# First mixer's shift and scale: fp32 products of two columns, or fp32r products of four columns of high and low parts

## The chip, the cores and the metric

One Trainium2 chip, one of its cores. The metric is the device time of one execution in microseconds (us); smaller is better. Several executions are timed, and one more is profiled.

## The reference

Two blocks of layers over 512 tokens of width 1024, with a context of 256 tokens beside them in the first. What matters here stands at the very start: a vector c (for the tokens) and a vector c_ctx (for the context) give the shift and the scale of the first mixer's input.

```
ada        = silu(c)     @ ada_w[0] + ada_b[0]     (1024 -> 12 x 512)
ada_ctx    = silu(c_ctx) @ ada_w[0] + ada_b[0]
modulate(t, shift, scale) = t * (1 + scale) + shift
h, hc      = modulate(x, ...), modulate(ctx, ...)
p, pc      = h @ w_in, hc @ w_in                   (then scans, convolutions, feed-forward, a second block)
```

Shift and scale of the first mixer are the column blocks q = 0..3 of `ada_w[0]` (q 0 and 1 shift, q 2 and 3 scale; an even q serves the first half of the 1024 features, an odd one the second half). All is float32. The dense layers of the kernel reach that with fp32r: each operand is cut into a high part (a cast) and a low part (the rest), and three products of parts are summed.

## The kernel before

**Order of the program.** `Kern.consts` (L343) sets constants and calls `ada_begin` (L598), which loads c and c_ctx, and takes silu into `sv`, 128 x 8 x 2: for each of 8 blocks k of 128 features one column for c and one for c_ctx. Then `mixer` (L1236) calls `modulated_inputs` (L679). A scheduler sets the order on each engine; `order` rows below show it. Each engine works through its own list in order, SP's list is the queue of most loads.

**The head.** `modulated_inputs` runs: `ada_head(2)`, `ada_head(0)`; loads of the first half of x and ctx (`load(0)`, L699); the weight loads of the first two dense layers, `dt` (`wdt`, 48 columns) and the first block of `wxbc` (128 columns, here called xbc8); `modulate(0)` (L702 to L711); `ada_head(1)` and `ada_head(3)` in turns; `load(1)`; the first four blocks of those two dense layers; `modulate(1)`.

**`ada_head(q)`** (L607) takes the weights of one q as four pairs of blocks, 128 x 1024 float32, 512 KB each. A pair lands in a buffer that is a `wraw`, a `wh` or a `wl` of the weight pool by turns (three of each, nine in all). For each of the 8 blocks one fp32 product, `sv[:, k]` (two columns) times 128 x 512 weights, sums into `pr` (2 x 512, L617). The sum goes to SBUF (`adarow`, L624), four small transposes turn it into columns (`pt`, L626), and two vector instructions add the bias into `hm` (L629).

**`modulate(half)`** for four blocks each: ScalarE makes t * scale + shift in place (L707), VectorE the same for the context (L709), ScalarE casts both to their high parts `ch` and `xh` (L710), VectorE and GpSimd (for the context) subtract for the low parts `xl` and `cl` (L711).

**The dense layers** (`dense2`, L737) load weights by `wload` (L381): land in `wraw`, ScalarE casts to `wh` (L394), VectorE and GpSimd subtract for `wl` (L396, L397). `mm3` (L403) makes the three products (L405 to L407). `wh` and `wl` have three buffers each, and a layer keeps its pair until the product of its last block, k = 7.

```
raw = self.wp.tile([P, 1024], F32, name="wraw", tag="wraw", bufs=3)
wh = self.wp.tile([P, 1024], F32R, name="wh", tag="wh", bufs=3)
wl = self.wp.tile([P, 1024], F32R, name="wl", tag="wl", bufs=3)
```

**After the head** `ssd_dt` (L770) takes the sum of `dt` through some 20 small steps on VectorE and ScalarE; TensorE's first instruction that needs it is the transpose `ptd` (L815). Meanwhile TensorE goes on with the other `wxbc` layers.

Of the kernel before, what the change touches and what calls it, by code (L numbers as in the profile page):

```python
# [10 lines left out]
F32 = mybir.dt.float32  # L11
F32R = mybir.dt.float32r
# [5 lines left out]
P = 128  # L18
T = 512
TC = 256  # L20
D = 1024
KD = 8
# [293 lines left out]
class Kern:  # L316
# [26 lines left out]
    def consts(self):  # L343
        nc, cst = self.nc, self.cst
# [5 lines left out]
        nc.gpsimd.affine_select(self.ident, self.ident, pattern=[[1, P]], base=0, channel_multiplier=-1,  # L350
                                compare_op=OP.is_equal, fill=0.0)
        self.ones = cst.tile([P, 1], F32, name="ones")
        nc.vector.memset(self.ones, 1.0)
# [244 lines left out]
    def ada_begin(self):  # L598
        nc = self.nc
        cv = self.cst.tile([P, KD, 2], F32, name="cv")  # L600
        nc.scalar.dma_start(cv, self.i["cvec"])
        self.sv = self.cst.tile([P, KD, 2], F32, name="sv")
        nc.scalar.activation(self.sv, cv, AF.Silu)
        self.m = [self.cst.tile([P, 48], F32, name=f"m{l}") for l in range(2)]
        self.mc = self.cst.tile([P, 16], F32, name="mc")

    def ada_head(self, q):  # L607

        nc = self.nc
        pr = self.x("pr")  # L610
        for k in range(0, KD, 2):
            self.nraw += 1
            raw = self.wp.tile([P, 1024], F32, name="wraw", tag=("wraw", "wh", "wl")[self.nraw % 3], bufs=3)
            nc.sync.dma_start(raw, self.i["ada0"][q, :, k:k + 2].rearrange("p k c -> p (k c)"))
            for j in range(2):
                r = raw[:, j * 512:(j + 1) * 512]
                nc.tensor.matmul(pr[:2], self.sv[:, k + j], r, start=k + j == 0, stop=k + j == KD - 1)  # L617
            yield
# [4 lines left out]
        row = self.t("adarow")  # L623
        nc.vector.tensor_copy(row[:2], pr[:2])  # L624
        for j in range(4):
            nc.tensor.transpose(pt[:, j], row[:2, j * P:(j + 1) * P], self.ident[:2, :2])  # L626
        hm = self.hm[q] = self.ctxp.tile([P, 2, 4], F32, name=f"hm{q}")
# [608 lines left out]
    def mixer(self):  # L1236
        nc = self.nc
# [11 lines left out]
        pb = self.pool("ssdb", 1, es=ess, **right)  # L1249
        chain = lambda *g: (c for x in g for c in x)  # L1250
        dt, s0 = self.dense2(self.i["wdt"], 0, 48), self.ssd_inputs(0, pa)
        self.modulated_inputs([dt, s0])
# [1285 lines left out]
```

## Time and profile before

| | |
|---|---|
| time, median of 3 runs | 2649.17 us (2646.44 to 2653.3) |
| the profiled execution | 2647.25 us, span of its trace 2645.5 us |
| TensorE (PE) busy | 2562.8 us, 97% of the span |
| VectorE (DVE), ScalarE (ACT), GpSimd (POOL) | 68%, 43%, 30% |
| DMA | 264.30 MB, mean 100 GB/s |

Rows of the trace name an engine, a source line (L617), the tiles written and read (out<-in), and a shape; times are in us from the span's start. "[0.76 <-DVE dtv L798]" is idle time of the engine before the row, and what ended it. A 128x512 fp32 product stands as two records in the trace.

### The profile page before, as it was taken

To read this page: it belongs to the slowest core of one execution; us is meant where nothing else is said; L and a number is where in the kernel's file an instruction comes from. 1 tells how busy PE (TensorE), PEld (TensorE's weight loads), DVE (VectorE), ACT (ScalarE), POOL (GpSimd) and SP (SyncE) were. 2 spreads that over 40 slices of the span, in tenths; PEclk is the share of its full clock that TensorE was granted. 3 is DMA by queue.
4 is the path that set the end of the run, shared out by engine and by line. 5 is a ranking of instruction groups with operands and counts; after the bars stand their busy time and mean duration, and the time that the engine had idled before them with its cause. 6 is when DMAs were issued, how large, how long until landed. Compare 5 with 4: busy or idle time off the path is not lost. (4 is left out here: it accounts for less than half of the span.)

```text
span 2645.5 us, 37506 instructions
## 1 busy us (share of the span) xinstructions
PE 2562.8 (97%) x14044; PEld 2163.8 (82%) x14044; DVE 1787.2 (68%) x3239; ACT 1128.8 (43%) x1958; POOL 786.1 (30%) x818
## 2 busy tenths in 40 slices
PE   8999999999999999999989999999999999999998
PEld 3877778989779888788888888888887889988887
DVE  3787866775777988868977888557544777644422
ACT  3545433333425333226875433226545445433322
POOL 2133312231343211325635221342234112322231
PEclk9999999999999999999989999999999999999999
DMA  7223225441353333752202333333223102333332
GB/s 257 70 68 116 72 79 165 132 132 48 110 185 105 96 96 95 252 178 75 78 1 64 112 96 96 96 95 100 67 72 91 33 9 80 113 98 99 97 94 76
DMA packets 94181, 264.30 MB, mean 100 GB/s; under 512 B 11008, under 2 KB 15424, under 8 KB 94000
## 3 DMA queue, kind: packets, MB, share of 16 engines
q1 hardware_dynamic: 87136, 249.00, 30.7%
q10 hardware_dynamic: 4752, 6.63, 0.7%
q0 software_dynamic: 2112, 6.29, 0.7%
q8 instruction: 110, 1.80, 0.3%
q14 instruction: 71, 0.58, 0.1%
HBM read 253.39 MB, written 7.44 MB: 99 GB/s over the span
## 5 line engine op out<-in xcount | busy, mean ns | idle before, releaser
L405 PE MATMUL acc<-xh,wl 128*128 128x512 f32 (+2 forms) x2056 | 778.0, 379 | 9.5 <-ACT xh L1624 3.1
L406 PE MATMUL acc<-xh,wh 128*128 128x512 f32 (+2 forms) x2056 | 767.8, 374 | 0.0
L407 PE MATMUL acc<-xl,wh 128*128 128x512 f32 (+2 forms) x2056 | 765.3, 375 | 1.1 <-POOL xl L379 0.8
L397 POOL TENSOR_TENSOR wl<-wraw,wh 128x256 fp32r<-128x256 f32 (+2 forms) x318 | 345.1, 1086 | 1158.4 <-ACT wh L394 1055.2
L394 ACT CAST wh<-wraw 128x1024 fp32r<-128x1024 f32 (+2 forms) x318 | 326.4, 1028 | 531.3 <-PE acc L407 318.2
L396 DVE TENSOR_TENSOR wl<-wraw,wh 128x768 fp32r<-128x768 f32 (+2 forms) x318 | 349.2, 1099 | 180.8 <-ACT wh L394 149.5
L405 PEld LDWEIGHTS acc<-xh,wl 128*128 128x128 f32 (+1 forms) x2056 | 392.1, 191 | 74.0 <-issue 4.7
L407 PEld LDWEIGHTS acc<-xl,wh 128*128 128x128 f32 (+1 forms) x2056 | 389.9, 191 | 72.0 <-issue 2.5
L406 PEld LDWEIGHTS acc<-xh,wh 128*128 128x128 f32 (+1 forms) x2056 | 392.1, 191 | 57.2 <-issue 1.9
L2456 DVE SCALAR_TENSOR_TENSOR cacc<-acc,pk,cacc 128x441 f32<-128x441 f32 (+2 forms) x352 | 243.8, 693 | 27.9 <-ACT cacc L2447 18.6
L405 PE MATMUL acc<-gh,wl 128*128 128x512 f32 (+1 forms) x594 | 221.9, 374 | 0.0
L407 PE MATMUL acc<-gl,wh 128*128 128x512 f32 (+1 forms) x594 | 221.1, 372 | 0.0
L406 PE MATMUL acc<-gh,wh 128*128 128x512 f32 (+1 forms) x594 | 220.7, 372 | 0.0
L642 DVE SCALAR_TENSOR_TENSOR adaacc<-adaraw,sv,adaacc 128x512 f32<-128x512 f32 x140 | 116.5, 835 | 31.7 <-DMA adaraw<-in_ada 29.7
L406 PEld LDWEIGHTS acc<-gh,wh 128*128 128x128 f32 x594 | 113.0, 190 | 21.4
L407 PEld LDWEIGHTS acc<-gl,wh 128*128 128x128 f32 x594 | 112.8, 190 | 21.3
L405 PEld LDWEIGHTS acc<-gh,wl 128*128 128x128 f32 x594 | 112.9, 190 | 21.0
L1543 DVE SCALAR_TENSOR_TENSOR pc<-up,pk,pc 128x512 f32<-128x512 f32 x119 | 89.7, 754 | 3.3
L2400 DVE SCALAR_TENSOR_TENSOR cacc<-acc,pk,cacc 128x511 f32<-128x511 f32 (+1 forms) x44 | 33.0, 750 | 70.0 <-ACT cacc L2398 69.2
L1138 ACT COPY kcur<-kk 128x512 f32<-128x512 f32 x56 | 37.3, 666 | 92.7 <-DVE kk L1162 92.6
L1148 PE MATMUL pa<-qq,kcur 128*128 128x128 f32 x448 | 64.6, 288 | 6.5 <-DVE qq L1160 6.3
L1164 POOL TENSOR_TENSOR tot<-tot 128x256 f32<-128x256 f32 (+5 forms) x48 | 26.9, 561 | 145.0 <-DVE qq L1160 134.6
(673 smaller groups left out, 4633.3 us busy)
## 6 DMA issues: line engine op xcount, KB each, us to landing
wraw<-in_wup SPq DMA_DIRECT2D x132, 512.0 KB, 3.6
adaraw<-in_ada SPq DMA_DIRECT2D x160, 256.0 KB, 3.4
wraw<-in_wdn SPq DMA_DIRECT2D x48, 512.0 KB, 3.6
wraw<-in_wc SPq DMA_DIRECT2D x24, 512.0 KB, 3.6
wraw<-in_wdn SPq DMA_DIRECT2D x24, 384.0 KB, 3.1
wraw<-in_ada SPq DMA_DIRECT2D x16, 512.0 KB, 5.7
wraw<-in_wf SPq DMA_DIRECT2D x16, 512.0 KB, 3.8
wraw<-in_wo SPq DMA_DIRECT2D x16, 512.0 KB, 3.7
```

The costliest lines, as they stand in the source:

```text
L394: nc.scalar.copy(wh[:, :n], raw[:, :n])
L396: nc.vector.tensor_sub(wl[:, :c], raw[:, :c], wh[:, :c])
L397: nc.gpsimd.tensor_sub(wl[:, c:n], raw[:, c:n], wh[:, c:n])
L405: mm(acc, wl, xh, start=first, stop=False)
L406: mm(acc, wh, xh, start=False, stop=False)
L407: mm(acc, wh, xl, start=False, stop=last)
L642: nc.vector.scalar_tensor_tensor(a, r, self.sv[:, k, 0:1], a, op0=OP.mult, op1=OP.add)
L1138: nc.scalar.copy(t.rearrange("p (a b c) -> p a b c", b=2, c=m), self.alt(kk, 0)(m))
L1148: mm(pa[:, s], kcur[:, s], self.alt(qq, 1)(m, c * P, P), start=True, stop=True)
L1543: nc.vector.scalar_tensor_tensor(pc, at(j0 + j), w(j0 + j, n), pc, op0=OP.mult, op1=OP.add)
L2400: nc.vector.scalar_tensor_tensor(a[:, d:], pg[:, :T - d], self.col("gcw", (2 - d) * KF + j), a[:, d:], op0=OP.mult, op1=OP.add)
L2456: nc.vector.scalar_tensor_tensor(o, g3[:, r0 + dy:r1 + dy, c0 + dx:c1 + dx], w, o, op0=OP.mult, op1=OP.add)
```

## The change

`sv4` holds for each block four columns: the high parts of the two, then their low parts. The weights of a pair are cut as those of a dense layer are: ScalarE casts each half (128 x 512) to `wh`, VectorE or GpSimd subtracts to `wl`; GpSimd takes the first half of the pairs k = 0 and k = 4, VectorE all else. Two fp32r products per block, of `wh` and of `wl` with all four columns, sum into `pr` (4 x 512). The four transposes become four products with `sel4`, 4 x 2, that also add the rows of high and low parts. Pairs now land in `wraw` alone, or (every second one) as two loads of 256 KB in two of the four `er` tiles, which the scan uses later.

```diff
+        self.sel4 = cst.tile([4, 2], F32, name="sel4")
+        nc.vector.tensor_add(self.sel4, self.ident[0:4, 0:2], self.ident[0:4, 2:4])
...
+        self.sv4 = self.cst.tile([P, KD, 4], F32R, name="sv4")
+        nc.scalar.copy(self.sv4[:, :, 0:2], self.sv)
+        nc.vector.tensor_sub(self.sv4[:, :, 2:4], self.sv, self.sv4[:, :, 0:2])
...
-            raw = self.wp.tile([P, 1024], F32, name="wraw", tag=("wraw", "wh", "wl")[self.nraw % 3], bufs=3)
-            nc.sync.dma_start(raw, self.i["ada0"][q, :, k:k + 2].rearrange("p k c -> p (k c)"))
+            if self.nraw % 2:
+                t = self.wp.tile([P, 1024], F32, name="wraw", tag="wraw", bufs=3)
+                nc.sync.dma_start(t, self.i["ada0"][q, :, k:k + 2].rearrange("p k c -> p (k c)"))
+                raw = t[:, :512], t[:, 512:]
+            else:
+                raw = [self.erp.tile([P, T], F32, name="er", bufs=4) for _ in range(2)]
+                for j in range(2):
+                    nc.sync.dma_start(raw[j], self.i["ada0"][q, :, k + j])
+            wh = self.wp.tile([P, 1024], F32R, name="wh", tag="wh", bufs=3)
+            wl = self.wp.tile([P, 1024], F32R, name="wl", tag="wl", bufs=3)
             for j in range(2):
-                r = raw[:, j * 512:(j + 1) * 512]
-                nc.tensor.matmul(pr[:2], self.sv[:, k + j], r, start=k + j == 0, stop=k + j == KD - 1)
+                s = slice(j * 512, (j + 1) * 512)
+                nc.scalar.copy(wh[:, s], raw[j])
+                (nc.vector if j or k % 4 else nc.gpsimd).tensor_sub(wl[:, s], raw[j], wh[:, s])
+                nc.tensor.matmul(pr[:4], self.sv4[:, k + j], wh[:, s], start=k + j == 0, stop=False)
+                nc.tensor.matmul(pr[:4], self.sv4[:, k + j], wl[:, s], start=False, stop=k + j == KD - 1)
...
-        nc.vector.tensor_copy(row[:2], pr[:2])
+        nc.vector.tensor_copy(row[:4], pr[:4])
         for j in range(4):
-            nc.tensor.transpose(pt[:, j], row[:2, j * P:(j + 1) * P], self.ident[:2, :2])
+            nc.tensor.matmul(pt[:, j], row[:4, j * P:(j + 1) * P], self.sel4, start=True, stop=True)
```

The list of ScalarE around the end of `modulate(0)`. Before (L710 casts of the last block, then at once what comes ahead of `modulate(1)`, L707 on `yc`; L800 belongs to `ssd_dt`):

```order
17 L707 ACTIVATE xin<-xin,hm_206,hm_179 128x512
18 L710 CAST ch<-xin 128x256
19 L710 CAST xh<-xin 128x512
20 L800 ACT_TABLE_LOAD
21 L800 ACTIVATE ea<-pk 48x1
22 L707 ACTIVATE yc<-yc,hm_325,hm_315 128x512
```

Of the change, with the semaphores that a row waits for in brackets (PE, DVE and Pool are other engines' progress, DMAHW a load; L724 and L727 are the lines of `modulate`, L631 the casts of `ada_head`):

```order
36 L727 CAST xh<-xin 128x512 [waits Activation_49]
37 L631 CAST wh<-wraw 128x512 [waits DMAHW3_49,PE_49]
38 L631 CAST wh<-wraw 128x512
39 L631 CAST wh<-er 128x512 [waits DVE_49,DMAHW4_49,PE_49,Pool_49]
40 L631 CAST wh<-er 128x512 [waits DMAHW5_49]
41 L631 CAST wh<-wraw 128x512 [waits DVE_49,DMAHW6_49,PE_49,Pool_49]
42 L631 CAST wh<-wraw 128x512
43 L631 CAST wh<-er 128x512 [waits DMAHW7_49,DVE_49,PE_49]
```

Sixteen casts of `ada_head(1)` and `ada_head(3)` now stand between the two halves of `modulate`, and the first cast of each pair waits for TensorE, VectorE or GpSimd as well as for its load.

TensorE in the same stretch, before (L617 the fp32 products, L405 to L407 those of `dt`):

```order
12 L617 MATMUL pr<-wraw,sv 2x512 x6
13 L405 MATMUL acc<-xh,wl 48x512
14 L406 MATMUL acc<-xh,wh 48x512
15 L617 MATMUL pr<-wraw,sv 2x512 x6
16 L407 MATMUL acc<-xl,wh 48x512
17 L405 MATMUL acc<-ch,wl 48x256
18 L406 MATMUL acc<-ch,wh 48x256
19 L617 MATMUL pr<-wraw,sv 2x512 x2
```

Of the change (L633 and L634 the new products, L407 to L409 those of the dense layers, 128 rows for xbc8):

```order
61 L633 MATMUL pr<-wh,sv_78 4x512
62 L408 MATMUL acc<-ch,wh 48x256
63 L409 MATMUL acc<-cl,wh 48x256
64 L634 MATMUL pr<-wl,sv_78 4x512
65 L633 MATMUL pr<-wh,sv_78 4x512
66 L407 MATMUL acc<-xh,wl 128x512
67 L408 MATMUL acc<-xh,wh 128x512
68 L634 MATMUL pr<-wl,sv_78 4x512
69 L409 MATMUL acc<-xl,wh 128x512
70 L633 MATMUL pr<-wh,sv_78 4x512
71 L407 MATMUL acc<-ch,wl 128x256
72 L408 MATMUL acc<-ch,wh 128x256
```

The products of `ada_head` now stand among the first halves of both dense layers, where before only half of `dt` stood among them.

TensorE behind the last transposes, before (the end of `dt`'s first half, then xbc8's first half, of which row 35 is the first product):

```order
30 L626 MATMUL pt<-ident,adarow 128x2 x4
31 L407 MATMUL acc<-xl,wh 48x512
32 L405 MATMUL acc<-ch,wl 48x256
33 L406 MATMUL acc<-ch,wh 48x256
34 L407 MATMUL acc<-cl,wh 48x256
35 L405 MATMUL acc<-xh,wl 128x512
```

Of the change:

```order
115 L643 MATMUL pt<-sel_87,adarow 128x2 x8
116 L407 MATMUL acc<-ch,wl 48x256
117 L408 MATMUL acc<-ch,wh 48x256
118 L407 MATMUL acc<-ch,wl 128x256
119 L409 MATMUL acc<-cl,wh 48x256
120 L408 MATMUL acc<-ch,wh 128x256
121 L407 MATMUL acc<-xh,wl 48x512
122 L408 MATMUL acc<-xh,wh 48x512
```

Behind the transposes nothing is left that needs only the first half of the inputs; `dt` and xbc8 then go side by side.

## Rows read from the trace of the kernel before

**Rows 1.** The page: span, and busy time of the engines.

```profile
span 2645.5 us, 37506 instructions
PE 2562.8 (97%) x14044; PEld 2163.8 (82%) x14044; DVE 1787.2 (68%) x3239; ACT 1128.8 (43%) x1958; POOL 786.1 (30%) x818
```

**Rows 2.** Stretches of the head: busy us of engines, granted clock, DMA share, GB/s.

```profile
core 0: us, PE busy (x) PEld busy (x) DVE busy (x) ACT busy (x) POOL busy (x), PEclk, DMA share, GB/s
0.00:20.00 20.00, 13.89 (x31) 2.74 (x32) 1.65 (x12) 1.50 (x2) 0.70 (x6) 1.00 0.92 341
20.00:46.00 26.00, 22.96 (x74) 5.97 (x72) 9.05 (x20) 9.40 (x17) 5.07 (x6) 1.00 0.90 323
46.00:60.00 14.00, 14.00 (x81) 11.37 (x80) 9.79 (x15) 10.81 (x17) 6.10 (x6) 1.00 0.27 84
60.00:74.00 14.00, 13.24 (x90) 11.03 (x88) 9.96 (x19) 6.64 (x9) 2.19 (x2) 1.00 0.19 58
74.00:82.00 8.00, 8.00 (x33) 7.21 (x34) 6.91 (x19) 3.61 (x9) 0.05 (x1) 0.57 0.43 132
```

**Rows 3.** Timeline of TensorE, the products of ada_head(2) and ada_head(0).

```profile
5.24 9.15 PE L617 MATMUL pr<-wraw,sv 128*2 128x512 f32 x16 [5.24 <-ACT sv L603]
15.56 7.03 PE L617 MATMUL pr<-wraw,sv 128*2 128x512 f32 x16
```

**Rows 4.** Timeline, from the last sum of ada_head(0) through modulate(0).

```profile
22.63 0.68 DVE L624 COPY adarow<-pr 2x512 f32<-2x512 f32 x1 [0.47 <-PE pr L617]
23.36 0.40 PE L626 MATMUL pt<-ident,adarow 2*128 2x2 f32 x4 [0.77 <-DVE adarow L624]
24.36 0.22 DVE L629 SCALAR_TENSOR_TENSOR hm<-pt,pk 128x4 f32<-128x4 f32 x2
24.55 0.81 ACT L707 ACTIVATE xin<-xin,hm,hm 128x512 f32<-128x512 f32 x1 [1.10 <-DVE hm L629]
25.27 0.39 ACT L710 CAST ch<-xin 128x256 fp32r<-128x256 f32 x1
25.56 0.61 ACT L710 CAST xh<-xin 128x512 fp32r<-128x512 f32 x1
26.08 0.81 ACT L707 ACTIVATE xin<-xin,hm,hm 128x512 f32<-128x512 f32 x1
```

**Rows 5.** Timeline, casts of the weights of dt and xbc8.

```profile
21.15 0.51 ACT L394 CAST wh<-wraw 128x384 fp32r<-128x384 f32 x1 [15.96 <-DMA wraw<-in_wdt]
22.40 1.04 ACT L394 CAST wh<-wraw 128x1024 fp32r<-128x1024 f32 x1 [0.74 <-DMA wraw<-in_wxbc]
```

**Rows 6.** Lines L391, L392, L379: 128x512 cast and subtractions, ns min/median/max.

```profile
L391 ACT CAST wh<-wraw x36: 508/617/626, 790.7 to 2620.3; 128x512 fp32r<-128x512 f32 x30, 128x384 fp32r<-128x384 f32 x6
L392 DVE TENSOR_TENSOR wl<-wraw,wh x36: 548/684/1778, 792.6 to 2620.9; 128x512 fp32r<-128x512 f32 x30, 128x384 fp32r<-128x384 f32 x6
L379 POOL TENSOR_TENSOR gl<-u,gh x27: 1307/1313/2023, 855.1 to 2503.8; 128x512 fp32r<-128x512 f32 x27
```

**Rows 7.** Timeline, subtractions of POOL and DVE that overlap.

```profile
27.26 0.74 POOL L711 TENSOR_TENSOR cl<-xin,ch 128x256 fp32r<-128x256 f32 x1 [0.81 <-ACT ch L710]
27.74 0.81 DVE L711 TENSOR_TENSOR xl<-xin,xh 128x512 fp32r<-128x512 f32 x1 [0.53 <-ACT xh L710]
...
53.08 0.96 DVE L396 TENSOR_TENSOR wl<-wraw,wh 128x768 fp32r<-128x768 f32 x1
53.12 1.51 POOL L397 TENSOR_TENSOR wl<-wraw,wh 128x256 fp32r<-128x256 f32 x1 [0.74 <-ACT wh L394]
```

**Rows 8.** Timeline, the end of ada_head(1) and (3), and modulate(1)'s start.

```profile
43.10 1.28 DVE L624 COPY adarow<-pr 2x512 f32<-2x512 f32 x2 [11.50 <-PE pr L617]
45.66 0.23 DVE L629 SCALAR_TENSOR_TENSOR hm<-pt,pk 128x4 f32<-128x4 f32 x2 [0.93 <-PE pt L626]
45.86 0.82 ACT L707 ACTIVATE yc<-yc,hm,hm 128x512 f32<-128x512 f32 x1 [1.94 <-DVE hm L629]
```

**Rows 9.** Timeline of TensorE: dt's second half, its end, xbc8's end, ptd.

```profile
50.39 0.39 PE L405 MATMUL acc<-xh,wl 128*48 128x512 f32 x1
50.62 0.39 PE L406 MATMUL acc<-xh,wh 128*48 128x512 f32 x1
...
54.46 0.28 PE L407 MATMUL acc<-cl,wh 128*48 128x256 f32 x1
...
58.78 0.40 PE L405 MATMUL acc<-xh,wl 128*128 128x512 f32 x1
64.75 0.57 PE L815 MATMUL ptd<-ident,dtv 48*128 48x48 f32 x6 [0.76 <-DVE dtv L798]
```

**Rows 10.** The page's DMA issues: size and median time to landing.

```profile
adaraw<-in_ada SPq DMA_DIRECT2D x160, 256.0 KB, 3.4
wraw<-in_ada SPq DMA_DIRECT2D x16, 512.0 KB, 5.7
```

More of the change, by code (lines that the diff above doesn't have):

```diff
@@ L1250, in mixer @@
         chain = lambda *g: (c for x in g for c in x)
+        self.erp = pa
         dt, s0 = self.dense2(self.i["wdt"], 0, 48), self.ssd_inputs(0, pa)
```

## The prediction

> **What bounds the kernel now.** I read the page first [rows 1]: TensorE is busy 97% of the span, so the kernel as a whole is bound by TensorE, and work taken off it is worth its full time only where TensorE is what the stage waits for. So next the stretches of the head [rows 2]. In 0 to 20 us TensorE is busy 13.89 of 20 and the DMA share is 0.92 (341 GB/s), in 20 to 46 us 22.96 of 26 and 0.90: two resources are near their limits, and the other engines nearly idle. From 46 us TensorE never stops for 14 us, and DMA falls to 0.27. Then the products themselves [rows 3]: sixteen records, eight fp32 products of ada_head(2), run from 5.24 to 14.39 us; the next sixteen take 7.03 us, 0.44 each. The first half of the inputs is modulated from 24.55 us, right behind the sum of ada_head(0) [rows 4], the second from 45.86 us, behind those of ada_head(1) and (3) [rows 8]. These two times are what the change can move; behind them everything follows.
>
> **What it removes.** 64 records of 0.44 us, 28 us of TensorE. In their place stand 64 fp32r products. The dense layers show such a product of 512 columns starting every 0.23 us (50.39, 50.62 [rows 9]): 14.7 us. So TensorE loses 13 us of work.
>
> **What it adds.** Each of the 16 pairs needs two casts on ScalarE (0.62 us each [rows 6], the second starting 0.52 us after the first, as 25.56 to 26.08 in [rows 4]) and two subtractions, on VectorE 0.68 (0.74 taken, for the gaps) or on GpSimd 1.31 [rows 6]. Nothing of this existed before, and it now stands between a landed weight and its product. `sel4`, the four-column `sv4`, and eight more DMA issues on SP are tiny and lie beside the wait for the first weights: no cost. If that cover were gone `sv4` alone would cost about 0.3 us.
>
> **Step A, ada_head(2) and (0).** Eight pairs are 4.2 MB, and the tables on ScalarE's queue 0.98 MB; at 341 GB/s [rows 2] the last lands at 15.2 us. But only five pairs have landing buffers (three `wraw`, two pairs of `er`) where nine had; the eighth's loads wait for the fourth pair's subtractions, at about 12.7 us (3.1 MB landed at 10.7, two casts, two subtractions), and 256 KB take 3.4 us when the queue is short, 5.7 when it is full [rows 10]: 16.1, with 15.2 and 18.4 as bounds. From there cast 1.14, subtraction 0.74, product 0.4, `adarow` 0.68, `pt` 0.40, half of `hm` 0.11, and 0.4 of gaps between engines: 3.9. modulate(0) starts at 20.0 (19.1 to 22.3), against 24.55: **4.5 us earlier**. Here TensorE was the limit, and loads take over.
>
> **Step B, modulate(0).** Four blocks at 1.53 us each (24.55 to 26.08 [rows 4]) are 6.1 us of ScalarE. The casts for `dt` and xbc8 lay before it, in ScalarE's idle time [rows 5]; now their weights land behind the others, and the order puts them into it: 1.5 us. So the first cast of ada_head(1) comes at 20.0 + 6.1 + 1.5 = 27.6 us.
>
> **Step C, ada_head(1) and (3).** This is where the change gives its gain back. `wh` and `wl` have three buffers; `dt` and xbc8 hold one each until their last block, which needs modulate(1), which needs these very sums. One `wh` and one `wl` are left for eight pairs, and the order's waits say the same: the first cast of each pair waits for the engines that read the pair before. So the pairs run one after the other. A pair with VectorE alone: cast 0.62, two subtractions 1.48, gaps 0.1: 2.2 us to the next cast. A pair whose first half GpSimd takes: cast 0.62, subtraction 1.31, then on TensorE a product's start 0.23 and a product's end 0.40, gaps 0.14: 2.7. Two sizes are uncertain there. GpSimd can be stretched by VectorE's subtraction of the other half: 1.51 for 256 columns where VectorE began 0.04 us sooner, 0.74 where GpSimd began sooner [rows 7], and 2.02 at most for 512 [rows 6]; that would make the pair 3.4. In this chain GpSimd begins 0.5 us sooner, so I take 2.7. The Trainium skill, "SBUF — State Buffer", section "Who interferes with whom", says that a VectorE instruction with two SBUF inputs and a reading GpSimd one block each other wholly, and that the first to start goes through. By that rule the pair is 2.7 as well, and 3.4 is excluded; but in the first overlap of rows 7 VectorE ended at 28.55, 0.55 behind GpSimd's end, less than its own 0.68, so the trace agrees on who wins and not on whole blocking, and I keep 3.4 as the bound.
> Four of each: 10.8 + 8.8 = 19.6, and 0.4 until the last product ends: 47.6 us. The bounds: 22.4 with the stretch, 18.8 with the shortest rows. Products of the dense layers' first halves, 8.4 us, fit into the same time on TensorE; loads don't matter, since a pair needs 2.5 us and 512 KB land every 1.5.
>
> **Step D.** Two `adarow` copies 1.28 [rows 8], `pt` 0.40, `hm` 0.23, gaps 0.2: modulate(1) starts at 49.7 us, against 45.86: **3.9 later** (2.2 to 9, all lower and all upper bounds).
>
> **Step E, behind it.** Before, TensorE had xbc8's first half still to do (4.1 us) while modulate(1) ran, and reached xbc8's end without a pause at 58.78, 12.9 us after modulate(1)'s start. Now that half is done; what is left is four blocks of each layer, 8.3 us, behind the first context block (ScalarE 1.1, GpSimd 0.8, gaps): 10.3. xbc8 ends at 60.0, 1.3 later. But `dt` now goes side by side with xbc8 and ends near 59.0, not at 54.74 [rows 9]. Its chain took 10.0 us to `ptd`, which TensorE already waited 0.76 us for [rows 9]. So `ptd` comes at 69.0, **4.3 late**; by the new order TensorE has some 1.5 us more work done then. Net 2.8 us, and no later stage has a reason to give it back at 97%.
>
> **The sum.** 2647.25 + 2.8 = 2650.1 for the profiled execution, which lies 1.9 under the median of the runs shown: **2652 us** as a median, 0.1% slower. That is within the 0.3% (7.9 us) that a measurement of this kernel can tell from no change. With the bounds alone 2650 to 2657; the order changes in the first tenth of the program, where waits like the 0.76 us come and go, and I give these 4 us either way.
>
> **Rivals.**
> *The clock falls in the head (slower).* Before, the granted clock was 1.00 until 74 us, and 0.57 in 74 to 82 us [rows 2] (the lower of its two levels, 1.2 GHz, for most of it); 8 us at 0.57 cost 3.4. Now TensorE has nothing from the last `pt` of ada_head(0) (19.5) to `dt`'s first product (23), and from the last product (47.6) to the first of modulate(1) (51). If the clock falls at both, the GpSimd pairs and the others lose about 0.4 us each, 3.2, and a stretch as long as the one at 74 costs 3.4 behind modulate(1): 2647.25 + 1.9 + 2.8 + 6.6 = 2658.6, slower. It decides from about 10 us of such work on the path. Against it: the pauses that the trace has until 46 us left the clock at 1.00. The Trainium skill, "TensorE: Matmul & The Clock Gate", section "HAM oscillation — how this bites in real kernels", says that a matmul stream broken by waits can fall back to the low clock at every wait; by that rule this case comes, and rows 2 show one fall, though TensorE was busy for 13.24 of the 14 us before it.
> *The pairs overlap after all (faster, but little).* If the buffers come free so that pairs follow at the pace of loads, 1.5 us, step C takes 12, modulate(1) starts at about 42, and the end is about 5 us earlier than before: 2644. For it speaks only that ScalarE could cast a pair in 1.04 us [rows 5]; the waits of the order speak against it.
> *TensorE's 13 us are saved whole (faster).* If the head were TensorE's alone, 2649.2 - 13 = 2636. For it: 97%. Against it: DMA at 0.90 and 0.92 [rows 2], and step C.
>
> **Chances.** Forecast 0.60, clock 0.22, overlap 0.12, whole saving 0.06. Faster by over 0.3%: 0.06. Slower: the clock's 0.22 and 0.03 for the forecast's upper tail, 0.25. The same: 0.69. The range takes in the forecast with its bounds, the clock's 2658.6 with some two us of order, and part of the overlap case: 2645 to 2661; what it leaves out is the whole saving, half of the overlap, and little of the clock.
>
> **What would show it.** Right: modulate(0) starts near 20 us and modulate(1) near 50; in between the first casts of L631 start 2.2 to 2.7 us apart and each waits for VectorE, GpSimd or TensorE; `ptd` near 69. Step A is wrong if modulate(0) starts after 23; step C if the casts start 1.5 us apart, or 3.4. A granted clock well under 1.00 before 60 us is the clock's case. The whole is wrong if modulate(1) starts before 45.

## The result and the profile after

The change makes the kernel slower: 2664.79 us as a median of 4 runs (2664.07 to 2667.72) beside 2651.24 of the kernel before on the same chip, a ratio of 1.0051 with a 95% interval of 1.0037 to 1.0064, or 13.5 us. The forecast was 2652 us with a range of 2645 to 2661.

Two lines of the page after; TensorE's busy time rose by 6.1 us against [rows 1], though 28 us of fp32 records went:

```profile
span 2663.7 us, 37659 instructions
PE 2568.9 (96%) x14060; PEld 2178.8 (82%) x14060; DVE 1804.9 (68%) x3265; ACT 1146.2 (43%) x1991; POOL 800.1 (30%) x826
```

The stretches of [rows 2], and four more, columns as there:

```profile
0.00:20.00 20.00, 8.97 (x29) 2.74 (x30) 10.73 (x24) 9.83 (x18) 5.99 (x10) 0.96 0.88 299
20.00:46.00 26.00, 19.67 (x80) 10.20 (x78) 13.85 (x22) 14.16 (x26) 9.32 (x9) 0.83 0.66 226
46.00:60.00 14.00, 9.12 (x38) 5.08 (x37) 7.88 (x15) 5.90 (x10) 2.02 (x2) 0.85 0.74 257
60.00:74.00 14.00, 13.77 (x60) 10.39 (x61) 8.03 (x12) 10.40 (x17) 6.52 (x7) 0.78 0.17 49
...
8.00:12.00 4.00, 3.44 (x8) 0.71 (x6) 1.95 (x5) 2.27 (x4) 1.10 (x1) 1.00 1.03 389
28.00:35.00 7.00, 5.37 (x17) 3.12 (x18) 5.60 (x8) 6.44 (x13) 5.18 (x6) 0.54 0.59 189
56.00:66.00 10.00, 8.54 (x31) 6.60 (x31) 5.20 (x13) 6.99 (x13) 3.06 (x4) 0.50 0.10 39
```

Over 20 to 60 us as a whole nothing is near a limit any more: TensorE is busy 28.8 of 40 us where it had 37.0, and the DMA share falls from 0.90 to 0.66 in 20 to 46. (From 47 to 56 us it is 0.94, with the second half of the inputs and the next weights of `wxbc`; no pair waits for these.) Such a stretch is set by waits. The granted clock falls too, to 0.57 in 18 to 22 us, 0.54 in 28 to 35 and 0.50 in 56 to 66, so that TensorE spends most of these stretches at the lower level.

Timeline around the two halves' joint: the sum of ada_head(2), its `pt`, the first and last product rows of ada_head(0), its sum, and modulate(0):

```profile
13.98 0.40 PE L634 MATMUL pr<-wl,sv 128*4 128x512 f32 x1
...
15.40 0.62 ACT L631 CAST wh<-er 128x512 fp32r<-128x512 f32 x1 [0.16 <-DMA er<-in_ada]
16.02 0.68 DVE L632 TENSOR_TENSOR wl<-er,wh 128x512 fp32r<-128x512 f32 x1
16.62 0.67 DVE L641 COPY adarow<-pr 4x512 f32<-4x512 f32 x1
17.35 1.05 PE L643 MATMUL pt<-sel,adarow 4*128 4x2 f32 x8 [2.97 <-DVE adarow L641]
18.32 0.57 PE L633 MATMUL pr<-wh,sv 128*4 128x512 f32 x1
...
19.83 1.14 ACT L631 CAST wh<-er 128x512 fp32r<-128x512 f32 x2 [1.91 <-PE pr L633]
...
23.36 0.40 PE L634 MATMUL pr<-wl,sv 128*4 128x512 f32 x1
23.79 0.68 DVE L641 COPY adarow<-pr 4x512 f32<-4x512 f32 x1 [2.02 <-PE pr L634]
25.81 0.81 ACT L724 ACTIVATE xin<-xin,hm,hm 128x512 f32<-128x512 f32 x1 [4.84 <-DVE hm L646]
```

TensorE's last product of ada_head(2) ends at 14.4 us. Then it stands 3.0 us at `pt`, which waits for a copy; the copy stands on VectorE's list behind a subtraction whose weights had just landed. All 16 products of ada_head(0) stand behind that `pt` and end at 23.8. They also hold the three `wh`: the casts of the last pair wait for them until 19.83, though its two loads, issued at 13.4 and 14.0 us, had landed 4.0 us later. modulate(0) starts at 25.81, 1.3 us later than before [rows 4], not 4.5 earlier.

Timeline of the second half: the first casts of the eight pairs of ada_head(1) and (3) (column 1 is the start), the last sum, and modulate(1):

```profile
33.30 1.13 ACT L631 CAST wh<-wraw 128x512 fp32r<-128x512 f32 x2
34.88 1.72 POOL L632 TENSOR_TENSOR wl<-wraw,wh 128x512 fp32r<-128x512 f32 x1
37.36 1.14 ACT L631 CAST wh<-er 128x512 fp32r<-128x512 f32 x2 [2.92 <-PE pr L633]
40.08 1.14 ACT L631 CAST wh<-wraw 128x512 fp32r<-128x512 f32 x2 [1.58 <-PE pr L633]
42.60 1.14 ACT L631 CAST wh<-er 128x512 fp32r<-128x512 f32 x2 [1.37 <-PE pr L633]
44.71 1.14 ACT L631 CAST wh<-wraw 128x512 fp32r<-128x512 f32 x2 [0.97 <-PE pr L633]
47.50 1.14 ACT L631 CAST wh<-er 128x512 fp32r<-128x512 f32 x2 [1.65 <-PE pr L633]
50.30 1.14 ACT L631 CAST wh<-wraw 128x512 fp32r<-128x512 f32 x2 [1.66 <-PE pr L633]
52.37 1.14 ACT L631 CAST wh<-er 128x512 fp32r<-128x512 f32 x2 [0.93 <-PE pr L633]
...
54.80 1.28 DVE L641 COPY adarow<-pr 4x512 f32<-4x512 f32 x2 [0.49 <-PE pr L634]
55.53 3.24 PE L643 MATMUL pt<-sel,adarow 4*128 4x2 f32 x16 [0.77 <-DVE adarow L641]
59.01 0.82 ACT L724 ACTIVATE yc<-yc,hm,hm 128x512 f32<-128x512 f32 x1 [3.99 <-DVE hm L646]
78.92 0.57 PE L832 MATMUL ptd<-ident,dtv 48*128 48x48 f32 x6 [0.32 <-DVE dtv L815]
```

Each pair but the first waits for TensorE's products of the one before: 2.07 to 2.11 us where VectorE alone subtracts (2.52 once), 2.72 to 2.80 where GpSimd takes a half, 4.06 for the first, where GpSimd was still at modulate(0) until 34.88. modulate(1) starts at 59.01 (45.86 before [rows 8]), `ptd` at 78.92 (64.75 [rows 9]): 14.2 us late. The products `pyy` of the second block, 1800 us further on, show the delay still there, 12.4 us at the first and 15.8 at the last; before, then after:

```profile
L1781 PE MATMUL pyy<-Tm,NT x160: 270/275/377, 1890.2 to 2198.6; 128*128 128x128 f32 x160
```

```profile
L1799 PE MATMUL pyy<-Tm,NT x160: 270/275/377, 1902.6 to 2214.4; 128*128 128x128 f32 x160
```

So the loss arises in the first 79 us and is handed on. The profiled spans differ by 18.2, more than the medians, since the profiled execution of before is one of its shorter ones (2647.25).

### The profile page after: what moved, and what is told of

Same layout as the page of the kernel before. It is cut to its first block, busy times and chain, and to the rows that moved or that the text cites. A ratio compares the mean times of both kernels' runs of the same rounds, so it can differ in the third digit from the quotient of the medians.

```text
span 2663.7 us, 37659 instructions
## 1 busy us (share of the span) xinstructions
PE 2568.9 (96%) x14060; PEld 2178.8 (82%) x14060; DVE 1804.9 (68%) x3265; ACT 1146.2 (43%) x1991; POOL 800.1 (30%) x826
## 5 line engine op out<-in xcount | busy, mean ns | idle before, releaser
L407 PE MATMUL acc<-xh,wl 128*128 128x512 f32 (+2 forms) x2056 | 781.6, 381 | 13.0 <-DVE wl L398 4.3
L409 PE MATMUL acc<-xl,wh 128*128 128x512 f32 (+2 forms) x2056 | 768.1, 376 | 1.1 <-POOL xl L381 0.8
L407 PEld LDWEIGHTS acc<-xh,wl 128*128 128x128 f32 (+1 forms) x2056 | 394.1, 192 | 76.9 <-DVE wl L398 4.8
L409 PEld LDWEIGHTS acc<-xl,wh 128*128 128x128 f32 (+1 forms) x2056 | 391.7, 192 | 72.7 <-issue 2.6
L407 PE MATMUL acc<-gh,wl 128*128 128x512 f32 (+1 forms) x594 | 220.7, 372 | 0.0
L409 PE MATMUL acc<-gl,wh 128*128 128x512 f32 (+1 forms) x594 | 219.8, 370 | 0.0
L409 PEld LDWEIGHTS acc<-gl,wh 128*128 128x128 f32 x594 | 112.1, 189 | 21.3
L407 PEld LDWEIGHTS acc<-gh,wl 128*128 128x128 f32 x594 | 112.0, 189 | 21.0
L1181 POOL TENSOR_TENSOR tot<-tot 128x256 f32<-128x256 f32 (+5 forms) x48 | 27.1, 565 | 145.6 <-DVE qq L1177 135.4
```

The source lines that it names most:

```text
L407: mm(acc, wl, xh, start=first, stop=False)
L409: mm(acc, wh, xl, start=False, stop=last)
```

## Experiments

Theory: chains of waits in the head, one pair after the other, hold it. Rivals: the fallen clock, the landing of weights. All runs, times in us from the span's start, from one traced execution each; each ratio is to the kernel before on the same chip:

| run | modulate(0) | modulate(1) | `ptd` | ratio to before, 95% interval |
|---|---|---|---|---|
| before | 24.55 | 45.86 | 64.75 | 1 |
| the change | 25.81 | 59.01 | 78.92 | 1.0051 (1.0037 to 1.0064) |
| half20 | 27.55 | 55.50 | 72.92 | 1.0029 (1.0018 to 1.0040) |
| half13 | 26.05 | 57.97 | 76.07 | 1.0033 (1.0021 to 1.0045) |
| land | 27.00 | 45.15 | 64.53 | 1.0004 (0.9995 to 1.0013) |
| warm | 29.11 | 69.66 | 86.57 | 1.0075 (1.0063 to 1.0088) |
| warm2 | 25.19 | 59.77 | 77.47 | 1.0037 (1.0024 to 1.0050) |
| bufs | 28.01 | 54.45 | 72.59 | 1.0020 (1.0007 to 1.0033) |
| dve | 24.91 | 53.07 | 72.80 | 1.0031 (1.0020 to 1.0041) |
| tland | 27.95 | 61.94 | 80.49 | 1.0041 (1.0025 to 1.0056) |
| late | 26.88 | 50.11 | 77.22 | 1.0046 (1.0033 to 1.0059) |
| late_tails | 25.21 | 48.61 | 77.59 | 1.0050 (1.0032 to 1.0067) |
| fix | 25.88 | 52.37 | 70.50 | 1.0014 (1.0002 to 1.0026) |
| bwarm | 23.38 | 47.65 | 66.05 | 1.0009 (0.9999 to 1.0020) |
| bufs_dve | 24.03 | 48.64 | 66.79 | 1.0008 (0.9996 to 1.0019) |
| bufs_dve_tails | 22.50 | 48.43 | 68.14 | 0.9996 (0.9986 to 1.0006) |
| dve_tails | 22.01 | 52.01 | 71.73 | 1.0016 (1.0005 to 1.0027) |
| fix_tails | 23.35 | 49.42 | 68.31 | 1.0012 (1.0002 to 1.0023) |

The end follows `ptd`, but only within some 5 us: 2 us late gives 1.0008, 8 us 1.0020 to 1.0031, 14 us 1.0051; `tland`, 15.7 us late at `ptd`, ends 11 us late, and `bufs_dve_tails`, 3.4 us late, 1 us early.

Two things limit what this table can tell. The time at which modulate(0) starts spreads by 2.1 us among runs with the same program up to there (the change 25.81, `late` 26.88, `half20` 27.55, `tland` 27.95); in the later ones more products of ada_head(0) start 0.43 us apart instead of 0.23, in `tland` those from 19.43 to 24.94 us, in the change those from 18.69 to 21.68. And executions of one kernel differ with the granted clock of the whole span: the 35 of the kernel before beside the last runs go from 2643.61 us at 0.987 to 2660.99 at 0.981, some 1.8 us for each 0.001. The change ran at 0.978 to 0.980, the kernel before at 0.983 to 0.984 as a mean beside the other runs. Part of that is the fall in the head itself; how much of the 13.5 us goes with the clock, these ratios don't say.

**half20: the change for q = 2 and 0 alone.**

```diff
+            if q in (2, 0):
...
             else:
+                raw = self.wp.tile([P, 1024], F32, name="wraw", tag=("wraw", "wh", "wl")[self.nraw % 3], bufs=3)
...
```

> ada_head(2) and (0) as in the change, ada_head(1) and (3) as before (fp32 products, landing in wraw, wh and wl by turns). Chain theory (each pair of ada_head(1) and (3) passes through one wh and one wl, one after the other, and the delay of modulate(1) passes to the end): modulate(0) as in the change, near 25.8 us (1.3 later than before); but ada_head(1) and (3) follow their loads again, so modulate(1) comes at 46 to 48 us instead of 59.0, ptd at 65 to 67, and the kernel ends 0 to 3 us behind before, 11 to 14 us ahead of the change. Clock theory (the falls of the granted clock cost the time, wherever they come): the pause in front of the first transposes and the one in front of dt's first product stay, so the clock falls at 18 and at 28 us as in the change, and at least half of the loss stays: 6 us or more behind before.

Missed: modulate(1) came at 55.5, not 46 to 48, and the kernel was 7.7 us slower. No pair is cut here, so it is another wait. SP's own waits up to 60 us, and its timeline:

```profile
SPq L386 <- DVE wl L398: 10.2, 1, 10.2
SPq L638 <- DVE wl L398: 7.8, 2, 7.0
```

```profile
21.46 13.24 SPq L638 DMA_DIRECT2D wraw<-in_ada  x5
...
37.69 5.31 PE L641 MATMUL pr<-wraw,sv 128*2 128x512 f32 x12 [1.28 <-DMA wraw<-in_ada]
```

SP needs 13.2 us for five loads: they wait for buffers that dt and xbc8 free only when their weights are cast and subtracted, and that now happens inside modulate(0), at 30 us instead of 21 to 22 [rows 5]. The second half has two limits, pairs and loads. The end is also the one that the clock theory gave (6 us or more behind). In the trace the granted clock is 0.94 and more from 34 us on, while the products wait for loads, so the late modulate(1) is the loads' work; before 34 us the clock had fallen as in the change, and this run doesn't price that.

**half13: the change for q = 1 and 3 alone** (the same edit with the two cases exchanged).

> The other half: ada_head(2) and (0) as before, ada_head(1) and (3) as in the change. Chain theory: modulate(0) at 24.5 us as before, the first cast of ada_head(1) 7.5 later at 32, the last product 21.5 after that, modulate(1) 3 to 4 later: 56 to 58 us; ptd at 75 to 78; the kernel ends 9 to 13 us behind before, so nearly the whole loss sits in this half. Clock theory: with the pause at 14 us gone the clock stays at 1.00 until 54 us, and half of the loss goes: 4 to 8 us behind before.

modulate(1) and `ptd` came as the chain theory said; the end, 8.7 us behind, lies between the two forecasts. The clock fell here too, at 27.7 us, with no pause at 14 us. The halves cost 7.7 and 8.7 us alone and 13.5 together.

**land: fp32 as before, landing as in the change.**

```diff
-            raw = self.wp.tile([P, 1024], F32, name="wraw", tag=("wraw", "wh", "wl")[self.nraw % 3], bufs=3)
+            if self.nraw % 2:
+                t = self.wp.tile([P, 1024], F32, name="wraw", tag="wraw", bufs=3)
...
+                raw = [self.erp.tile([P, T], F32, name="er", bufs=4) for _ in range(2)]
```

> The kernel before, with fp32 products of two columns, but with the landing buffers of the change alone (pairs in wraw or in two er tiles, so five landing buffers in place of nine, wh and wl left to the dense layers). Chain theory: landing buffers were not what held the change up; modulate(0) at 24.5 to 26, modulate(1) at 46 to 49, the end 0 to 3 us behind before. Landing theory (loads that wait for buffers make the delay): modulate(1) later than 52 us and the end 6 us or more behind before.

The landing buffers alone cost nothing that can be told. And modulate(0) came 2.5 us later than before while modulate(1) came 0.7 sooner: in the kernel before, the start of modulate(0) did not set that of modulate(1), which fits a second half bound by its loads.

**warm and warm2: filler products in TensorE's pauses.** The first line is that of `warm` (zeros, 4 rows, into `pt`'s bank), the second that of `warm2` (128 rows, into a bank of its own).

```diff
+            nc.tensor.matmul(pt[:4, 64:], self.sv4[:, 0], self.z[:, 64:], start=True, stop=True)
...
+            self.nc.tensor.matmul(self.wacc, self.mean128, r, start=True, stop=True)
```

> The change, with products of a tile of zeros (448 columns, into unused columns of pt's bank) in TensorE's pauses ahead of and behind the small products pt: 10 ahead of ada_head(2)'s, 4 ahead of and 15 behind ada_head(0)'s, 3 and 3 ahead of those of (3) and (1), 9 behind (1)'s. Nothing waits for them but TensorE's own order. Both theories: the granted clock stays near 1.00 up to 66 us. Clock theory: then the loss is gone, modulate(0) at 21 to 23, modulate(1) under 51, and the kernel ends within 3 us of before. Chain theory: the clock is a part only: the 12 products of ada_head(0) at 0.43 us instead of 0.23 give back 2.4 us, the pt products 1.5, the dense products behind modulate(1) 2 to 3; modulate(0) at 23.4 to 24, modulate(1) at 54 to 56, and the kernel still ends 6 to 10 us behind before.

> The change, with filler products on TensorE that no one reads: stationary a 128x128 constant, moving a tile of ones (11 of them, from about 2.5 us until the first weights are cut) or the last pair's high part (10 ahead of ada_head(2)'s pt, 4 ahead of and 13 behind ada_head(0)'s, two per block in the last four pairs, 3 and 3 ahead of the last two pt, 7 behind). Unlike those of the run with zeros they have 128 rows, write a bank of their own that no copy waits for, and start before the first weights. They are TensorE's cheapest cover against the falls of the clock. If the clock costs a part only (chain theory): products of ada_head start 0.23 us apart from 8 us on, modulate(0) at 23 to 24 us instead of 25.8 (8 slow products and a slow last pair, some 2 us), modulate(1) at 54 to 56 instead of 59.0, ptd at 72 to 75 instead of 78.9, the end 4 to 7 us ahead of the change and still 6 to 10 behind before. Clock theory: modulate(1) under 51 and the end within 3 us of before.

`warm` was no clean test: the instruction that reads `pt` (`hm`) had to wait 3.93 us for the filler written to the same tile, and the clock fell all the same (0.50 in 53 to 70 us). In `warm2` the clock holds (columns as in [rows 2]):

```profile
16.00:48.00 32.00, 27.80 (x132) 16.36 (x131) 18.64 (x29) 16.55 (x31) 11.58 (x11) 1.00 0.73 244
48.00:84.00 36.00, 33.46 (x183) 24.80 (x181) 25.40 (x45) 21.58 (x32) 9.81 (x9) 1.00 0.38 123
```

Yet modulate(0) gains 0.6 us, modulate(1) nothing, `ptd` 1.5; the gains that the chain theory had forecast (2, 3 to 5 and 4 to 7 us) did not come either. With the clock at 1.00 from 16 to 84 us the loss stays, so the clock is not what makes most of it. The run bounds the clock's part only roughly: in the last pairs casts waited up to 2.35 us for filler.

**bufs, dve and bufs_dve: two pairs under way, no GpSimd, both.** The first two lines are those of `bufs`, the others those of `dve`.

```diff
+                if self.nraw % 2 == 0:
+                    wh, wl, s = self.t("awh", F32R), self.t("awl", F32R), slice(0, 512)
...
-                (nc.vector if j or k % 4 else nc.gpsimd).tensor_sub(wl[:, s], raw[j], wh[:, s])
+                nc.vector.tensor_sub(wl[:, s], raw[j], wh[:, s])
```

> The change, but every second pair of ada_head keeps its high and low parts in four 128x512 tiles of the kernel's small work buffers instead of a wh and a wl, so two pairs can be under way where one could. Pair theory (modulate(1) is late because ada_head(1) and (3) pass one pair after the other through one wh and one wl): the first casts of these pairs start 1.5 to 2.0 us apart instead of 2.1 to 2.8, modulate(1) comes at 52 to 54 us instead of 59.0, and the end is 5 to 7 us ahead of the change. Load theory (their loads stand in SP's queue behind a wraw buffer that dt and xbc8 hold until their casts inside modulate(0), so weights come too late anyway, as in the run with fp32 products in this half, which had modulate(1) at 55.5): modulate(1) no earlier than 55, the end 0 to 4 us ahead of the change.

> The change, with all subtractions of ada_head on VectorE and none on GpSimd. Pair theory: in the second half the first casts start 2.0 to 2.2 us apart throughout, and the first pair, which took 4.1 because GpSimd was still at modulate(0)'s subtractions, takes 2.5; that is 1.6 and four times 0.65 less, 3.5 to 4.5 us: modulate(1) at 54.5 to 56 where modulate(0) stays at 25.8, the end 3 to 5 us ahead of the change. If GpSimd's share lies beside other waits, modulate(1) comes at 58 or later.

> The change with two pairs under way and all subtractions on VectorE, without filler products. Each alone brought ptd from 78.9 to some 72.7 us. If they act on the same chain (pairs one after the other through one wh and wl, stretched by GpSimd), they do not add: the first casts of ada_head(1) and (3) start 1.3 to 1.7 us apart, modulate(1) at 49 to 52, ptd at 68 to 71, the end 2 to 6 us behind before. If they acted on different things, ptd comes at 66.5.

Each takes 6 us off `ptd`, both 12.1 of the 14.2, and with both the kernel is no slower than before by any measurable amount. Casts of `dve`, second, third and last pair, then of `bufs_dve`, the first two pairs and the last:

```profile
35.06 1.14 ACT L631 CAST wh<-er 128x512 fp32r<-128x512 f32 x2 [1.52 <-PE pr L633]
37.13 1.14 ACT L631 CAST wh<-wraw 128x512 fp32r<-128x512 f32 x2 [0.93 <-PE pr L633]
...
47.73 1.14 ACT L631 CAST wh<-er 128x512 fp32r<-128x512 f32 x2 [0.93 <-PE pr L633]
```

```profile
31.51 1.14 ACT L634 CAST wh<-wraw 128x512 fp32r<-128x512 f32 x2
32.55 1.14 ACT L634 CAST awh<-er 128x512 fp32r<-128x512 f32 x2
...
41.66 1.14 ACT L634 CAST awh<-er 128x512 fp32r<-128x512 f32 x2
```

From the first cast to the last are 19.1 us in the change, 15.3 in `dve`, 10.2 in `bufs_dve`. From modulate(0) to modulate(1): 33.2 in the change, 28.2, 26.4 in `bufs`, 24.6 with both, so there they act on one chain as expected. That `ptd` adds up all the same comes from modulate(0), which differs between these runs (28.0 in `bufs`, 24.0 with both): in `bufs` the products of ada_head(0) ran 0.43 us apart, at the lower level, until 25 us. Nor is the clock the same: in `bufs_dve` it is 1.00 from 34 us on, in `dve` 0.90 from 40 to 73 us. Shorter waits and the higher clock come together here, and the runs don't part them.

**tland: ada_head(1) lands apart from dt and xbc8.**

```diff
+            if q == 1:
+                raw = [self.t("aland") for _ in range(2)]
```

> The change, but the pairs of ada_head(1) land in two 128x512 work buffers each instead of a wraw, so SP's queue no longer stands behind dt's and xbc8's wraw; their casts, wh and wl are left as in the change. Load theory: the loads of ada_head(1) and (3) are issued from 21 us on without a stop, and modulate(1) comes 3 us or more sooner than in the change, at 56 us or before. Pair theory: the loads land early and then wait; the first cast stays at 33, casts 2.1 to 2.8 apart, modulate(1) at 57.5 to 59.5, the end within 2 us of the change.

As the pair theory said, counted from modulate(0): 34.0 us to modulate(1) against 33.2. Loads are not the limit while the pairs are serial. (modulate(0) itself came 2.1 us later: `pt` started at 17.94 instead of 17.35, and the products behind it ran 0.43 us apart until 24.9 instead of 21.7.)

**late and late_tails: dt and xbc8 behind the pairs; in the second, ada_head(2)'s `pt` behind ada_head(0)'s products.**

```diff
-        for g in first:
-            next(g)
         modulate(0)
...
         for g in first:
-            for _ in range(4):
+            for _ in range(5):
```

(The later `pt` is the edit shown with the next runs.)

> The change, with the weight loads of dt and xbc8 and all their products put behind ada_head(1) and (3): neither their wh and wl nor their wraw stand in the way of the pairs. Both theories say that this takes away the second half's loss: modulate(0) as in the change (25 to 26 us), the first cast of ada_head(1) 6.1 later (32), pairs 1.5 to 1.8 apart, modulate(1) at 47 to 50, ptd at 67 to 71, the end 1 to 5 us behind before. Clock theory: the pauses get longer, the clock falls more, the end is 8 us or more behind before.

> As the run before, and the sum of ada_head(2) goes to SBUF and through pt only behind all products of ada_head(0), so that TensorE does not stand at pt while the products behind it are ready. Theory of the first half (modulate(0) is 5.8 us later than forecast because TensorE's list stood 3.0 us at ada_head(2)'s pt, which waited for a copy that stood behind a subtraction on VectorE's list, and the clock fell there): no pause at 14.4 us, the clock at 1.00 until modulate(0), modulate(0) at 21 to 23, modulate(1) at 44 to 46.5, the end within 2 us of before or up to 3 ahead. If loads or buffers set the first half instead, modulate(0) stays at 24.5 or later.

modulate(1) comes 9 to 10 us sooner than in the change, yet the kernel is hardly faster: `ptd` stays at 77. The first halves of dt and xbc8, which lay beside the pairs, now stand behind them, and modulate(1) to `ptd` takes 27.1 us instead of 19.9. Both missed their forecast of the end, and the clock theory's number (8 us or more behind) came. But in `late` TensorE stands 5.05 us for `dt`'s weights, until 54.93 us, and of the products behind that only the first eight start at the lower level's pace, some 1.3 us in all. The time of modulate(1) alone was the wrong thing to aim at. In `late_tails` modulate(0) stayed at 25.2, not at the 21 to 23 expected. Twelve products started 0.43 us apart, from 13.18 to 17.83 us, 2.1 us more than at 0.23, and a subtraction of GpSimd took 4.28 us; TensorE stood 0.70 us for that one. GpSimd's list, VectorE's, and the product that waited:

```profile
17.03 4.28 POOL L632 TENSOR_TENSOR wl<-wraw,wh 128x512 fp32r<-128x512 f32 x1 [1.02 <-ACT wh L631]
17.09 1.27 DVE L632 TENSOR_TENSOR wl<-er,wh 128x512 fp32r<-128x512 f32 x2
18.29 0.67 DVE L632 TENSOR_TENSOR wl<-wraw,wh 128x512 fp32r<-128x512 f32 x1
18.89 1.28 DVE L632 TENSOR_TENSOR wl<-er,wh 128x512 fp32r<-128x512 f32 x2
...
21.36 0.40 PE L634 MATMUL pr<-wl,sv 128*4 128x512 f32 x1 [0.70 <-POOL wl L632]
```

**bufs_dve_tails, dve_tails: the later `pt` without GpSimd** ("the run before" is `bufs_dve`).

```diff
-        self.drain(self.ada_head(2))
-        self.drain(self.ada_head(0))
+        a, b = self.ada_head(2), self.ada_head(0)
+        for g in (a, b):
+            for _ in range(4):
+                next(g)
+        self.drain(a)
+        self.drain(b)
```

> As the run before, and ada_head(2)'s sum is copied and sent through pt behind all products of ada_head(0). If modulate(0) is late because the 16 products of ada_head(0) stand behind that pt on TensorE, they now run as their weights come: no pause of TensorE at 14 to 17 us, modulate(0) at 21 to 23 instead of 25.8, even at 0.43 us a product; modulate(1) 2 to 4 us sooner than in the run before, the end 0 to 4 us behind before. If loads set it, modulate(0) stays at 24.5 or later.

> The change with all subtractions on VectorE and with ada_head(2)'s pt behind ada_head(0)'s products, one pair under way. Here one pt still stands ahead of the last seven products by the scheduler's order. modulate(0) at 22 to 24 against 24.9 with VectorE alone, casts of the second half 2.0 to 2.2 us apart, modulate(1) at 50 to 52.5, ptd 1 to 3 us ahead of that run (72.8).

Step A's cause is borne out: modulate(0) moves to 22.5 and 22.0, outside all that runs with the early `pt` gave (24.0 to 29.1). Of the 2.9 us that `dve_tails` gains on `dve`, some 1.6 are the clock: eight products that started 0.43 us apart in `dve` (18.99 to 22.24) start 0.23 apart. The 1.5 us of `bufs_dve_tails` hold no such change in those products. In all four pairs of runs that differ in the place of that `pt` (`late`, `dve`, `bufs_dve` and `fix`, each with its `_tails`), modulate(0) comes 1.5 to 2.9 us sooner. In `bufs_dve_tails` the products run without the pause, `pt` last:

```profile
16.57 0.60 PE L637 MATMUL pr<-wl,sv 128*4 128x512 f32 x1
...
20.01 0.39 PE L637 MATMUL pr<-awl,sv 128*4 128x512 f32 x1
20.33 1.94 PE L646 MATMUL pt<-sel,adarow 4*128 4x2 f32 x16
```

But modulate(1) moves by 0.2 us only (48.43 against 48.64), and in `dve_tails` by 1.1: what is won in the first half is partly lost to the second half's own waits. In `bufs_dve_tails` these are the loads, as the last pairs show:

```profile
39.10 1.14 ACT L634 CAST wh<-wraw 128x512 fp32r<-128x512 f32 x2 [1.26 <-DMA wraw<-in_ada]
...
42.15 0.62 ACT L634 CAST awh<-er 128x512 fp32r<-128x512 f32 x1 [1.38 <-DMA er<-in_ada]
```

**fix, fix_tails and bwarm: filler added to the repairs, and to the kernel before.** The first two have `warm2`'s filler on top of `bufs_dve` and `bufs_dve_tails` (in `fix_tails` none ahead of ada_head(2)'s `pt`); `bwarm` has this ahead of the first product of the kernel before:

```diff
+        for _ in range(11):
+            nc.tensor.matmul(acc, self.mean128, z, start=True, stop=True)
```

> All repairs at once: two pairs under way (half of the pairs in small work buffers), all subtractions on VectorE, filler products on TensorE. If the chain of the head is understood, each takes its part away: modulate(0) at 22 to 24, the first cast of ada_head(1) 7.5 later, casts 1.4 to 1.8 us apart, modulate(1) at 46 to 49, ptd at 65 to 68, the end within 3 us of before and 10 to 14 us ahead of the change. If something else holds the head (loads, SP's queue), modulate(1) stays at 52 or later.

> Two pairs under way, VectorE alone, the later pt, and filler products on TensorE (none ahead of ada_head(2)'s pt). If clock and order are the first half's only limits beside loads: products 0.23 us apart from 8 us on, modulate(0) at 20.5 to 22.5 (the forecast's 20.0 at last), modulate(1) at 47 to 50, ptd at 65 to 68, the end within 3 us of before. If filler products stand in the way themselves, modulate(1) comes later than without them.

> The kernel before (fp32 products), with 11 filler products of a 128x128 constant and a tile of ones ahead of its first product. Its first six fp32 records start 0.81 to 0.85 us apart and all later ones 0.43: TensorE begins at the lower of its two levels, though the view of the granted clock shows 1.00 there. If the filler raises the clock earlier, the first records start 0.43 apart by 7 us at the latest, modulate(0) comes 1 to 2.5 us sooner (22 to 23.5), and since the second half is bound by loads, modulate(1) at 44.5 to 46, the end 0 to 2 us ahead of before: less than can be told. If not, nothing moves by over 0.5 us.

Filler never paid: `fix` has `ptd` later than the same repairs without it (70.5 against 66.8), `fix_tails` at the same time (68.3 against 68.1). `fix` missed its forecast, with modulate(1) at 52.4 instead of 46 to 49, a number that it had given to loads or SP's queue; without filler the same repairs have it at 48.6. In `bwarm` modulate(0) gains 1.2 us, and modulate(1) comes 1.8 later. No version here is faster than the kernel before; `bufs_dve` and `bufs_dve_tails` are level with it.

## Why the prediction was wrong

The sign of the likeliest case was right (slower) and so was its mechanism, a head bound by serial pairs; its size was a third of what came (4.3 us late at `ptd` instead of 14.2; at the end 2.8 instead of 13.5). `ptd` was forecast at 69.0 and came at 78.9; the 9.9 us between, by the forecast's steps:

- **Step A, +5.8: the step that failed.** "Loads take over" and modulate(0) at 20.0, or 22.3 at most; it came at 25.8. The sum left only the last pair's product behind the last load. It overlooked where ada_head(2)'s `pt` stands on TensorE's list: 16 products wait behind it, and it waits for a copy behind a subtraction on VectorE's list. I read the order only for the second half. By the rows of the change, the last pair's first cast came at 19.83 instead of 16.1. Of these 3.7 us, 1.8 went by until a load had landed and ScalarE was free (17.92, inside the forecast's bounds), and 1.9 in a wait for products behind that `pt`. Behind the cast come 1.6 us of clock (eight of the products started 0.43 us apart instead of 0.23), which the forecast proper had left out, and 0.65 for the eight records of `pt` (1.05 instead of 0.40). With the `pt` moved behind the products, modulate(0) gains 1.5 us (`bufs_dve_tails`) to 2.9 (`dve_tails`, with the clock's 1.6). It then comes at 22.0 to 22.5, near the forecast's upper bound and not at its 20.0.
- **Step B, -0.1.** modulate(0) to the first cast took 7.5 us, forecast 7.6.
- **Step C, +1.5.** From the first cast to the last product's end 21.5 us, forecast 20.0. Pairs of 2.1 and 2.7 to 2.8 are right to 0.1; the first pair, 4.06, had GpSimd still busy with modulate(0), which no term counted.
- **Step D, +2.1.** 4.2 us from the last product to modulate(1) instead of 2.1. I priced `pt` by [rows 4] at 0.40 for four records. With `sel4` one q has eight records, 1.05 us at 17.35, and the two q's at the lower clock took 3.24, 1.1 more than twice 1.05. The diff shows the product in place of the transpose; the doubling was not seen.
- **Step E, +0.6.** modulate(1) to `ptd` took 19.9 us, forecast 19.3. (By its own figures xbc8's end was to come 1.2 us later than before, not 1.3.) The 1.5 us that TensorE was to be ahead did not show: the delay at the first `pyy` is 12.4 and at the last 15.8, around the 14.2 at `ptd`.

Two small points of step A: 341 GB/s bring 3.1 MB by 9.1 us, not 10.7; the kernel before moved 194 GB/s in the first 5 us, 371 in the next and 406 behind them, which does give 10.7. And `sv4`, put at no cost, held the first product until 7.28 us, since its subtraction took 1.24 us; from 10.88 TensorE waits for casts of weights again, so that was made up.

**The rivals.** The clock did fall, well under 1.00 before 60 us, and its 2658.6 was the nearest of the numbers given; but `warm2` held the clock and the loss stayed. By the rows above its share at `ptd` is some 3 us (1.6 in step A, 1.1 in step D, part of step E), an estimate for this one execution; no run isolates it. The Trainium skill, "TensorE: Matmul & The Clock Gate", section "HAM oscillation — how this bites in real kernels", says that a stream of products broken by waits falls back to the low clock; the trace after agrees (0.50 in 56 to 66 us), but these rows put no more than those 3 us on it. Overlapping pairs (`bufs_dve`) bring level time, where that rival had 5 us of gain, and the change does not overlap them. TensorE's 13 us were not saved: it stood in waits.

**Where the expected gain of fp32r went.** TensorE's 13 us lay beside loads and waits; in their place came two casts and two subtractions in front of every product, which in the second half had one buffer pair to pass through.

## What to carry to other kernels

Where a step puts a cast and a subtraction between a load and its product, count the buffers that are left for the parts, and the share of the slowest engine in one pass through them: two pairs under way and no GpSimd took 8.6 us out of the second half here, and with an earlier modulate(0) 12 of the 14 us at `ptd`. Read the list of the bounding engine for every small instruction that waits for another engine, and sum what stands behind it. A part that is sooner (modulate(1) in `late`) is worth nothing if the work that lay beside its wait now follows it.

## What the runs showed of the hardware

**The clock at the start.** In the stretch 8 to 12 us of the change the view gives 1.00, but the products start 0.43 us apart there; two rows:

```profile
8.95 0.63 PE L633 MATMUL pr<-wh,sv 128*4 128x512 f32 x1
9.38 0.63 PE L634 MATMUL pr<-wl,sv 128*4 128x512 f32 x1
```

From 18.69 to 21.68 us, where the view gives 0.57 (18 to 22 us), they start 0.43 us apart too, and at 36.65 and 36.88, where it gives 1.00, 0.23. So TensorE begins at the lower level, and the view's 1.00 is no reading so early. `bwarm` bears this out: behind 4.2 us of filler the first records of the kernel before start 0.43 us apart from 6.74 us on, instead of 0.85. By the starts of its products it rose near 9.5 us in the kernel before (records some 0.85 us apart until then, 0.43 after), near 11 in the change and 25 in `bufs`. The forecast took the 1.00 until 74 us at its word.

**GpSimd beside VectorE.** Rows 17.03 to 18.89 of `late_tails`: a subtraction that takes 1.27 us alone took 4.28 while VectorE, which began 0.06 us later, did five of its own. The Trainium skill, "SBUF — State Buffer", section "Who interferes with whom", says that the one that issues first goes through whole. In the change the trace agrees: GpSimd's subtraction at 45.47 us took 1.27, and VectorE's, which began 0.41 us later, 1.40 instead of 0.68. In `late_tails` it does not: GpSimd, first by its record, took some 3 us longer than alone while instructions that began later ran. Spans on GpSimd are rough in this view, and 0.06 us is a small lead, so why it differs is not shown. GpSimd beside a busy VectorE cannot be costed by its own row alone.
